# A gated decoder layer on one core: weight sums in halves of 512 KB, and a new place in memory for the tiles that TensorE reads

## The chip, the cores and the metric

The kernel runs on one core of one Trainium2 chip. The time is the device time of one execution in microseconds; the kernel before took 329.92 us (median of 3 runs, 329.75 to 330.6).

## The reference

One pre-norm decoder layer on 256 tokens of width 1024, in float32, with three branches side by side.

```python
h = rms_norm(x, norm_g[layer])
(qa, ka, va, ga, ub, vb, gb, qc, gc, ma, mb, mc) = split_cols(h @ w_in[layer], IN_SPLITS)
out_a = moba_attention(qa, ka, va) * jax.nn.silu(ga)          # 6 heads of 128, causal, partial rotary
out_b = gmlp_spatial_gate(ub, vb, ...) * jax.nn.silu(gb)      # 6 groups of 128 channels
out_c = memory_cross_attention(qc, mem_n, w_mem_kv[layer]) * jax.nn.silu(gc)   # 4 heads, 256 memory tokens
y = (jax.nn.sigmoid(ma) * (out_a @ w_branch_a[layer])
     + jax.nn.sigmoid(mb) * (out_b @ w_branch_b[layer])
     + jax.nn.sigmoid(mc) * (out_c @ w_branch_c[layer]))
x = x + y @ w_out[layer]
return rms_norm(x, final_norm_g)
```

The combined projection `w_in` is 1024 x 8704. With it come a memory projection (1024 x 1024), the three branch projections (2048 x 1024 together) and the output projection (1024 x 1024).

## The kernel before, in words

**Chunks.** All weights pass through TensorE as a row of chunks of 128 x 1024 float32. The list `PLAN` names them: `mvk` (memory keys and values), `tok` (some values by token), `fea` (features: queries, keys, gates), `st` (products, below), `br` (branch projections), and at the end `out`. Two chunks that follow each other are one piece of 128 x 2048, 1 MB.

**Split numbers.** Each matmul is made of several in a fast float32 format (fp32r). ScalarE copies a chunk into `hi` (L258), which rounds it; VectorE subtracts that from the chunk and gets `lo` (L262). `hi` and `lo` are rings of five chunks, the split is issued four chunks ahead of the matmuls (`LEAD`). Activations are split the same way: `n` (the normed input), `s` (sums of its blocks), `m` (memory), `ah`/`al`, `obh`/`obl`, `och`/`ocl` (the branches' outputs) and `y`. Each holds a high and a low part. A product of `x` and `w` is `xh*hi + xh*lo + xl*hi`. In `tok`, `st`, `br` and `out` the activation is the stationary operand and `hi` or `lo` streams past in 512 columns; in `fea` the weights are stationary and `n` streams, 512 columns for `hi` (high and low part side by side) and 256 for `lo`.

**Products.** For five groups of 1024 columns (`g` = 0 to 4) a 2 x 2 block scheme makes seven products instead of eight, in the order 1, 2, 5, 3, 6, 7, 4. The weights of a product are a block of the matrix or a sum of blocks, and stand in one of two buffers of 1 MB, `form0` and `form1` (for odd `g` the two change places). Products 1, 5, 6, 4 use one buffer one after the other: block 0 is loaded (L226, SP's queue), then blocks 1, 3 and 2 are added to it in turn. Products 2, 3, 7 use the other: blocks 2 and 3 are loaded, then block 1 is added. An addition is a DMA that accumulates into the buffer (L229, POOL's queue). For groups 0 to 2 product 6 is made otherwise: VectorE adds the other buffer, which holds block 3 for product 3, over all 2048 columns at once (L240). A load or an addition can start only when the product before it in the same buffer has been split, so it waits for the last `lo` of that chunk.

**Order.** The order is written by a small planner at build time (`Units`). The chunks set a beat; at each chunk the planner issues the DMAs due there (`dma`, by the chunk at which a buffer comes free, `free`), then small units of attention, norms and gates where an engine has room, then the split of the chunk four ahead, then the matmuls. Each engine then works through its own list in that order and waits on semaphores. Products 1 to 7 of groups 0 to 2 and the first three of group 3 stand between feature chunks. The last eleven stand between the branch chunks: after the first two `br` chunks products 3 and 6 of group 3, after the next two product 7, then 4 and (group 4) 1, then 2 and 5, then 3 and 6, then 7, then 4. Two `br` chunks are 24 matmuls.

**Where tiles begin.** Pools are laid out one after the other, each tile at a multiple of 32 bytes in a partition. In the built program the bytes at which the tiles begin are, modulo 128: `m`, `s`, `n`, `y`, `obh`, `obl`, `och`, `ocl` at 96 (between bytes 45664 and 92768), `ah` (113280), `al` (127616 and 133760), `hi` (160384) and `lo` (180864) at 0, `ones` at 64 and its partner `dg` at 0. The tile `wspb` of 3096 bytes is what sets the tiles behind it apart from those ahead of it. All offsets inside these tiles are multiples of 512 bytes.

Of the kernel before, what the change touches and what calls it, by code (L numbers as in the profile page):

```python
# [24 lines left out]
F32 = mybir.dt.float32  # L25
# [3 lines left out]
OP = mybir.AluOpType  # L29
# [55 lines left out]
class Units:  # L85
# [29 lines left out]

    def fits(self, u, i, pe, now):
        name, e, us, fn, after, wait, due = u
        due = min([due] + [self.pe[a] + 4 for a in after if a in self.pe])
        if pe != (e == PE) or any(a not in self.end for a in after):
            return False  # L120
        if i >= due or e is None:
            return True
        if pe:
            return self.ready(after) + self.margin <= now
        if e == QUEUE:

            return self.ready(after) <= now
        lead = 0.5 if e == POOL else max(0.3, self.room - (2.4 if e == ACT else 1.3) - self.ahead - us)
        return self.t[e] <= now + lead and self.ready(after) <= max(now, self.t[e]) + 0.3

    def slot(self, i, pe):

        now, u = self.t[PE], True
        while u:
            if pe:
                now = self.t[PE]
            u = next((u for u in self.todo if self.fits(u, i, pe, now)), None)
            if u:
                self.todo.remove(u)
                name, e, us, fn, after, wait, due = u  # L140
                if e == PE:
                    self.pe[name] = i
                at = self.ready(after)
                self.end[name] = (at if e is None else self.run(e, us, at)) + wait
                fn()
# [3 lines left out]
def tile_hybrid_layer(ctx: ExitStack, tc: tile.TileContext, mw, xT, mem, x, fin_g, ln_g, w, ws, w_sp, b_sp, rope, out):  # L149
# [30 lines left out]
        return slice(h * 128, (h + 1) * 128)  # L180


    RAW, SPL, LEAD, JT = 3, 5, 4, 2
    raw, hi, lo = {}, {}, {}
    chunks = []
# [23 lines left out]

    def load(j):  # L210
        raw_alloc(j)
        parts = 2 if 18 <= j < 47 else 1
        for i in range(parts):
            load_part(j, i * PIECE // parts, (i + 1) * PIECE // parts)

    def block(g, i):

        return bass.AP(tensor=ws.tensor, offset=ws.offset + (4 * g + i) * 128 * PIECE, ap=[[PIECE, 128], [1, PIECE]])

    def form_tile(i):  # L220
        if f"form{i}" not in V:
            V[f"form{i}"] = (wts if i == 0 else act).tile([128, PIECE], F32, name=f"form{i}", tag=("f0", "mr")[i])
        return V[f"form{i}"]

    def form_load(i, g, b):
        nc.sync.dma_start(form_tile(i), block(g, b))  # L226

    def form_add(i, g, b):
        nc.gpsimd.dma_start(form_tile(i), block(g, b), accum_op=OP.add)  # L229


    SUMS = (0, 1, 2)
    FORMS = {1: (0, 0), 5: (0, 1), 6: (0, 3), 4: (0, 2), 2: (1, 2), 7: (1, 1), 3: (1, 3)}

    def buf(g, i):
        return FORMS[i][0] ^ (g % 2)

    def form_sum(i, g, b):

        nc.vector.tensor_tensor(form_tile(i), form_tile(i), form_tile(1 - i), OP.add)  # L240
        U.run(DVE, 2.35)

    def form_step(g, i):

        if i == 6 and g in SUMS:
            return form_sum, buf(g, i), g, 3

        return (form_add if i in (5, 6, 4, 7) else form_load, buf(g, i), g, FORMS[i][1])

    def split_alloc(c):  # L250
        if "hi" not in V:
            for n in ("hi", "lo"):
                V[n] = wts.tile([128, SPL, CH], F32R, name=n, tag=n)
        hi[c], lo[c] = V["hi"][:, c % SPL, :], V["lo"][:, c % SPL, :]

# [438 lines left out]
        nc.sync.dma_start(V["lng"], rows(ln_g, BW))  # L694

    def load_wsp():
        t = slot_tile("wspb", [128, GB * 128 + GB], "trig")
        nc.sync.dma_start(t, w_sp)
        V["wsp"], V["bst"] = t[:, 0:GB * 128].rearrange("p (g t) -> p g t", g=GB), t[:, GB * 128:]

    def cut_wsp():
        for g in range(GB):
# [439 lines left out]
        nc.sync.dma_start(out[:, t, 512:D], z[:, 512:D])  # L1142


    dma, ready, free = {}, {}, [6, 9]
    for c in range(n_br):
        if chunks[c][0] == "st" and chunks[c][3] == 0:
            b = buf(*chunks[c][1:3])
            at = free[b] + (chunks[c][2] not in (5, 6, 4, 7))
            if chunks[c][2] == 6 and chunks[c][1] in SUMS:  # L1150
                at = free[1 - b]
            dma.setdefault(at, []).append(form_step(*chunks[c][1:3]))
            ready[c // 2] = at
            free[b] = c + 2 - LEAD
    pace = lambda c: 5.0 + sum(SPAN.get(k[0], 2.73) for k in chunks[:c])
    for c, at in ready.items():
        i = chunks[2 * c][2]
        ready[c] = pace(at) + (2.5 if i == 6 and chunks[2 * c][1] in SUMS else 10.0 if i in (4, 5, 6, 7) else 6.0)
    for c in range(n_br + 4):
        now[0] = c  # L1160
        if c == n_br:
            nc.scalar.preload_act_table(AF.Sqrt)
            residual_parts()
        if c == n_br - 8:
            load_x()
        s = c + (LEAD if c > 9 else 3)
        for fn, *args in dma.pop(c, []):
            fn(*args)
        U.room = sum(SPAN.get(k[0], 2.73) for k in chunks[c:c + LEAD])
        U.slot(c, False)  # L1170
        if c in (7, 8):
            split_lo(2 * c - 6)
            U.end[f"s{2 * c - 6}"] = U.run(DVE, 1.23, U.t[ACT])
        for e in {5: (), 6: (), 7: (9,), 8: (11,), 9: (12, 13)}.get(c, (s,) if s > 3 else ()):
            if chunks[e][0] == "st":
                raw[e // 2] = form_tile(buf(*chunks[e][1:3]))
                came = ready[e // 2]
            else:
                came = {4: 24.0, 5: 25.5}.get(e // 2, 0.0)
            (split_mvk if e < KD else split)(e)  # L1180
            U.end[f"s{e}"] = U.run(DVE, 1.23, U.run(ACT, 1.05, max(U.end.get(f"c{e - SPL}", 0), came)))
        if c in (6, 7):
            split_alloc(2 * c - 4)
            split_hi(2 * c - 4)
            U.run(ACT, 1.05, (23.5, 28.0)[c - 6])
        s += c == 9
        if s % 2 == 1 and s // 2 in PLAIN:
            q = PLAIN.index(s // 2) + 2
            if 4 < q < len(PLAIN):
                load(PLAIN[q])  # L1190
            if q == 6:
                load_mem()
        kind = chunks[c][0]
        U.end[f"c{c}"] = U.run(PE, SPAN.get(kind, 2.73), U.end.get(f"s{c}", 0.0))
        if kind == "mvk":
            mm_mvk(c)
        elif kind == "tok":
            mm_tok(c)
        elif kind == "fea":
            mm_fea(c)  # L1200
        elif kind == "br":
            mm_br(c)
        elif kind == "st":
            mm_st(c)
        else:
            mm_out(c, 0)
            for a, b in (((0, 256), (256, 512)) if chunks[c][1] else ((0, 512),)):
                mm_out(c, 1, a, b)
        U.slot(c, True)
# [115 lines left out]
```

## Time and profile before

| | |
|---|---|
| median of 3 runs | 329.92 us |
| the profiled execution | 333.19 us, its span 331.5 us |
| granted TensorE clock, mean | 0.979 |
| TensorE busy | 317.0 us, 96% of the span |
| VectorE busy | 255.5 us, 77% |
| ScalarE busy | 226.8 us, 68% |
| GpSimd busy | 25.0 us, 8% |
| moved by DMA | 77.24 MB |

The span reaches from the first to the last instruction; the execution's own time is 1.7 us longer. A row of a group gives the line, the engine, the operation, the tile written and the tiles read, then the number of instructions, their busy time, the mean of one, and the idle time of the engine just before them with what ended it. "PEld" is the loading of TensorE's stationary operand. Some matmul records are missing from a trace, so times between matmuls are taken from their starts.

### The profile page before, as it was taken

The page shows a single profiled execution, that of the slowest core. Times are in us where ns is not written, and L with a number is a line of the kernel's source. Part 1 is how long each engine was busy: PE and PEld are TensorE (multiplying, and loading weights), DVE is VectorE, ACT ScalarE, POOL GpSimd, SP SyncE. Part 2 cuts the span into 40 slices and gives each one's busy share as a digit, 9 for nine tenths or more (in the row PEclk, how much of TensorE's full clock was granted, in tenths as well). Part 3 has the DMA queues.
Part 4 walks back from the last instruction along what each step waited for, and adds up shares of the span by engine and source line. Part 5 has one row for each costly group of instructions (what it writes and reads, how often), then busy time and mean ns, then how long its engine had stood idle before and what let it go on. Part 6 is the DMA issues. An engine that isn't in the chain of part 4 may idle for free. (4 is left out here: it accounts for less than half of the span.)

```text
span 331.5 us, 4343 instructions
## 1 busy us (share of the span) xinstructions
PE 317.0 (96%) x1542; PEld 261.6 (79%) x1542; DVE 255.5 (77%) x369; ACT 226.8 (68%) x357; POOL 25.0 (8%) x42
## 2 busy tenths in 40 slices
PE   7999999999999999999999999989999897999992
PEld 3888888888888888888888888867887675878882
DVE  2889989977698986975986999846982939889532
ACT  3877979547977869779957967819672744487333
POOL 1000030020010011022011010111010111000022
PEclk9999999999999999999999999997999797999997
DMA  7999998669669489869659789898799697943003
GB/s 205 407 401 417 406 284 288 228 150 190 245 217 259 156 257 213 280 223 222 207 190 173 225 334 211 253 265 165 264 312 292 173 266 133 378 175 128 2 0 127
DMA packets 16294, 77.24 MB, mean 233 GB/s; under 512 B 2064, under 2 KB 3088, under 8 KB 9744
## 3 DMA queue, kind: packets, MB, share of 16 engines
q1 hardware_dynamic: 13680, 59.00, 48.3%
q0 software_dynamic: 2448, 17.83, 28.4%
q8 instruction: 12, 0.20, 0.2%
q10 hardware_dynamic: 144, 0.13, 0.1%
q14 instruction: 10, 0.08, 0.1%
HBM read 75.12 MB, written 1.05 MB: 230 GB/s over the span
## 5 line engine op out<-in xcount | busy, mean ns | idle before, releaser
L262 DVE TENSOR_TENSOR lo<-form,hi 128x1024 fp32r<-128x1024 f32 x70 | 84.1, 1219 | 35.9 <-ACT hi L258 35.5
L258 ACT ACTIVATE hi<-form 128x1024 fp32r<-128x1024 f32 x70 | 72.2, 1056 | 44.8 <-DMA form<-in_ws_dram 33.3
L262 DVE TENSOR_TENSOR lo<-raw,hi 128x1024 fp32r<-128x1024 f32 x58 | 70.0, 1221 | 12.6 <-ACT hi L258 12.2
L258 ACT ACTIVATE hi<-raw 128x1024 fp32r<-128x1024 f32 x58 | 60.8, 1058 | 14.1 <-PE acc L448 4.7
L628 PE MATMUL acc<-n,hi 128*128 128x512 f32 x240 | 61.3, 397 | 0.0
L628 PEld LDWEIGHTS acc<-n,hi 128*128 128x128 f32 x240 | 43.7, 188 | 9.0
L229 POOL DMA_DIRECT2D form<-in_ws_dram x17 | 14.9, 876 | 255.4 <-DVE lo L262 151.0
L568 PE MATMUL acc<-hi,s 128*128 128x512 f32 x96 | 33.1, 403 | 0.0
L628 PEld LDWEIGHTS acc<-n,lo 128*128 128x128 f32 x240 | 30.9, 188 | 1.5
L628 PE MATMUL acc<-n,lo 128*128 128x256 f32 x240 | 31.9, 283 | 0.0
L568 PE MATMUL aux<-hi,s 128*128 128x512 f32 x64 | 24.0, 440 | 2.5 <-ACT hi L258 2.5
L568 PE MATMUL acc<-hi,n 128*128 128x512 f32 x72 | 25.3, 408 | 0.0
L568 PEld LDWEIGHTS acc<-hi,s 128*128 128x128 f32 x96 | 18.0, 188 | 4.2
L568 PE MATMUL acc<-lo,s 128*128 128x512 f32 x48 | 18.9, 394 | 0.0
L568 PEld LDWEIGHTS aux<-hi,s 128*128 128x128 f32 x64 | 13.5, 211 | 6.5 <-ACT hi L258 3.3
L568 PE MATMUL aux<-lo,s 128*128 128x512 f32 x32 | 14.6, 457 | 3.9 <-DVE lo L262 3.9
L568 PE MATMUL aux<-hi,n 128*128 128x512 f32 x48 | 15.9, 395 | 0.0
L568 PEld LDWEIGHTS acc<-hi,n 128*128 128x128 f32 x72 | 13.5, 188 | 3.0
L568 PE MATMUL acc<-lo,n 128*128 128x512 f32 x36 | 14.2, 394 | 0.0
L568 PEld LDWEIGHTS aux<-lo,s 128*128 128x128 f32 x32 | 6.6, 206 | 6.9 <-DVE lo L262 5.5
L568 PEld LDWEIGHTS aux<-hi,n 128*128 128x128 f32 x48 | 9.0, 187 | 2.2
L568 PEld LDWEIGHTS acc<-lo,s 128*128 128x128 f32 x48 | 9.0, 188 | 1.9
(233 smaller groups left out, 578.9 us busy)
## 6 DMA issues: line engine op xcount, KB each, us to landing
raw<-in_w_dram SPq DMA_DIRECT2D x18, 1024.0 KB, 8.7
form<-in_ws_dram POOLq DMA_DIRECT2D x17, 1024.0 KB, 9.7
form<-in_ws_dram SPq DMA_DIRECT2D x15, 1024.0 KB, 5.0
raw<-in_w_dram SPq DMA_DIRECT2D x22, 512.0 KB, 7.2
st<-in_mw_dram SPq DMA_DIRECT2D x7, 384.0 KB, 7.5
raw<-in_w_dram SPq DMA_DIRECT2D x8, 256.0 KB, 7.3
xk<-in_x_dram SPq DMA_DIRECT2D x2, 512.0 KB, 7.5
xt<-in_xT_dram SPq DMA_DIRECT2D x2, 512.0 KB, 8.6
```

Of the source, the lines that this page charges most:

```text
L229: nc.gpsimd.dma_start(form_tile(i), block(g, b), accum_op=OP.add)
L258: nc.scalar.activation(hi[c][:, a:b], raw[c // 2][:, o + a:o + b], AF.Copy)
L262: nc.vector.tensor_tensor(lo[c][:, a:b], raw[c // 2][:, o + a:o + b], hi[c][:, a:b].bitcast(F32), OP.subtract)
L568: nc.tensor.matmul(p, x[:, k0 + k, tsl(t)], wt[c][:, a * 512:(a + 1) * 512], start=first and a + j == 0, stop=half == 1 and a + j == 3, sk ...
L628: nc.tensor.matmul(o, wt, m, start=i == 0, stop=i == len(passes) - 1, skip_group_check=True)
```

## The change

Four edits, all in one file.

1. **Sums by halves.** Every load and every addition of a `form` buffer is issued for 1024 columns (512 KB) at a time, each half as soon as that half of the buffer is free. Product 6 is made by VectorE in all five groups, in two halves of 1024 columns.
2. **Where tiles begin.** `wspb` gets 3200 bytes instead of 3096, so `ah`, `al` and `hi` now begin at 96 modulo 128, as `n`, `s`, `m`, `y`, `obh`, `obl`, `och`, `ocl` do. A pad of 64 bytes stands ahead of `lo`, which begins at 32 modulo 128, 64 bytes apart from the others (`LOPAD = 16` floats). `ones` stays at 64, `dg` moves to 32.
3. **The planner.** The due time of a unit that follows a matmul is bound differently, for ScalarE and TensorE units.
4. Raw weight pieces 47 and 48 are loaded in two parts as well.

```diff
     def fits(self, u, i, pe, now):
-        due = min([due] + [self.pe[a] + 4 for a in after if a in self.pe])
+        due = due if pe else min([due] + [int(self.pe[a]) + 4 for a in after if a in self.pe])
...
+                up = [self.pe[a] for a in after if a in self.pe and self.pe[a] % 1 == 0]
                 if e == PE:
                     self.pe[name] = i
+                elif up and e == ACT:
+                    self.pe[name] = up[0] + 0.5
...
+    LOPAD = 16
...
-        parts = 2 if 18 <= j < 47 else 1
+        parts = 2 if 18 <= j < 49 else 1
...
-    def form_load(i, g, b):
-        nc.sync.dma_start(form_tile(i), block(g, b))
-
-    def form_add(i, g, b):
-        nc.gpsimd.dma_start(form_tile(i), block(g, b), accum_op=OP.add)
-    SUMS = (0, 1, 2)
+    def form_half(i, h):
+        return form_tile(i)[:, h * CH:(h + 1) * CH]
+
+    def form_load(i, g, b, h):
+        nc.sync.dma_start(form_half(i, h), block(g, b, h))
+
+    def form_add(i, g, b, h):
+        nc.gpsimd.dma_start(form_half(i, h), block(g, b, h), accum_op=OP.add)
+
+    def form_sum(i, g, b, h):
+
+        nc.vector.tensor_tensor(form_half(i, h), form_half(i, h), form_half(1 - i, h), OP.add)
+        U.run(DVE, 1.23)
...
-        if i == 6 and g in SUMS:
-            return form_sum, buf(g, i), g, 3
-        return (form_add if i in (5, 6, 4, 7) else form_load, buf(g, i), g, FORMS[i][1])
+    HOW = {5: (form_add, 8.0), 7: (form_add, 8.0), 4: (form_add, 8.0), 6: (form_sum, 1.5)}
...
-            for n in ("hi", "lo"):
+            for n, pad in (("hi", 0), ("lo", LOPAD)):
+                if pad:
+                    wts.tile([128, pad], F32, name=n + "pad", tag=n + "pad")
                 V[n] = wts.tile([128, SPL, CH], F32R, name=n, tag=n)
...
-        t = slot_tile("wspb", [128, GB * 128 + GB], "trig")
-        nc.sync.dma_start(t, w_sp)
+        t = slot_tile("wspb", [128, GB * 128 + 32], "trig")
+        nc.sync.dma_start(t[:, 0:GB * 128 + GB], w_sp)
...
-    dma, ready, free = {}, {}, [6, 9]
+    dma, ready, free = {}, {}, [[6, 6], [9, 9]]
...
+        if chunks[c][0] == "st":
+            _, g, i, h = chunks[c]
+            b = buf(g, i)
+            fn, us = HOW.get(i, (form_load, 5.0))
+            at = free[1 - b][h] if i == 6 else free[b][h] + (i not in HOW)
+            dma.setdefault(at, []).append((fn, b, g, FORMS[i][1], h))
+            ready[c] = pace(at) + us
+            free[b][h] = c + 1 - LEAD
```

VectorE's list around products 3 and 6 of group 3, where `form_326` (`form0`) holds block 3 and `form_400` (`form1`) becomes the sum; before:

```order
L262 TENSOR_TENSOR lo<-form_326,hi 128x1024
L673 TENSOR_TENSOR ub<-ub,jt 128x512
L262 TENSOR_TENSOR lo<-form_326,hi 128x1024
L1023 TENSOR_TENSOR ub<-ub,mt_1768 128x512
L262 TENSOR_TENSOR lo<-form_400,hi 128x1024 x2
L262 TENSOR_TENSOR lo<-raw,hi 128x1024
```

and now (the buffers' numbers are 327 and 402; the split's line L262 is now L264):

```order
L675 TENSOR_TENSOR ub<-ub,jt 128x512
L264 TENSOR_TENSOR lo<-form_327,hi 128x1024
L240 TENSOR_TENSOR form_402<-form_402,form_327 128x1024
L264 TENSOR_TENSOR lo<-form_327,hi 128x1024
L240 TENSOR_TENSOR form_402<-form_402,form_327 128x1024
L1025 TENSOR_TENSOR ub<-ub,mt_1781 128x512
L264 TENSOR_TENSOR lo<-form_402,hi 128x1024 x2
```

Two half sums have come in, one behind each half of product 3.

VectorE's list around products 3 and 6 of group 4, where the buffers have changed places and four evictions of branch b (L1075, L1077) stand between the halves of product 6; before:

```order
L262 TENSOR_TENSOR lo<-form_400,hi 128x1024 x2
L262 TENSOR_TENSOR lo<-form_326,hi 128x1024
L1075 TENSOR_TENSOR sigs_1855<-acc,sigs_1855 128x512
L1077 TENSOR_TENSOR sig_1462<-sig_1462,sigs_1855 128x512
L1075 TENSOR_TENSOR sigs_1855<-acc,sigs_1855 128x512
L1077 TENSOR_TENSOR sig_1462<-sig_1462,sigs_1855 128x512
L262 TENSOR_TENSOR lo<-form_326,hi 128x1024
```

and now:

```order
L264 TENSOR_TENSOR lo<-form_402,hi 128x1024
L240 TENSOR_TENSOR form_327<-form_327,form_402 128x1024
L264 TENSOR_TENSOR lo<-form_402,hi 128x1024
L240 TENSOR_TENSOR form_327<-form_327,form_402 128x1024
L264 TENSOR_TENSOR lo<-form_327,hi 128x1024
L1077 TENSOR_TENSOR sigs_1890<-acc,sigs_1890 128x512
L1079 TENSOR_TENSOR sig_1480<-sig_1480,sigs_1890 128x512
```

The two half sums stand ahead of the evictions, as the splits of product 3 did.

In POOL's list 30 additions of 128x1024 stand where 17 of 128x2048 stood, the two halves of a product next to each other; the two additions for product 6 of groups 3 and 4 are gone. SP's list has 30 loads of 128x1024 for 15 of 128x2048, nearly all side by side.

More of the change, by code (lines that the diff above doesn't have):

```diff
@@ L211, in load, with block @@
         raw_alloc(j)
-        parts = 2 if 18 <= j < 47 else 1
+        parts = 2 if 18 <= j < 49 else 1
         for i in range(parts):
             load_part(j, i * PIECE // parts, (i + 1) * PIECE // parts)
-    def block(g, i):
-        return bass.AP(tensor=ws.tensor, offset=ws.offset + (4 * g + i) * 128 * PIECE, ap=[[PIECE, 128], [1, PIECE]])
+    def block(g, i, h):
+        return bass.AP(tensor=ws.tensor, offset=ws.offset + (4 * g + i) * 128 * PIECE + h * CH, ap=[[PIECE, 128], [1, CH]])
     def form_tile(i):
@@ L236, in buf @@
         return FORMS[i][0] ^ (g % 2)
[L238 to L243, printed above, removed]
-        if i == 6 and g in SUMS:
-            return form_sum, buf(g, i), g, 3
-        return (form_add if i in (5, 6, 4, 7) else form_load, buf(g, i), g, FORMS[i][1])
+    HOW = {5: (form_add, 8.0), 7: (form_add, 8.0), 4: (form_add, 8.0), 6: (form_sum, 1.5)}
     def split_alloc(c):
         if "hi" not in V:
-            for n in ("hi", "lo"):
+            for n, pad in (("hi", 0), ("lo", LOPAD)):
+                if pad:
+                    wts.tile([128, pad], F32, name=n + "pad", tag=n + "pad")
                 V[n] = wts.tile([128, SPL, CH], F32R, name=n, tag=n)
@@ L696, in load_wsp @@
     def load_wsp():
-        t = slot_tile("wspb", [128, GB * 128 + GB], "trig")
-        nc.sync.dma_start(t, w_sp)
-        V["wsp"], V["bst"] = t[:, 0:GB * 128].rearrange("p (g t) -> p g t", g=GB), t[:, GB * 128:]
+        t = slot_tile("wspb", [128, GB * 128 + 32], "trig")
+        nc.sync.dma_start(t[:, 0:GB * 128 + GB], w_sp)
+        V["wsp"], V["bst"] = t[:, 0:GB * 128].rearrange("p (g t) -> p g t", g=GB), t[:, GB * 128:GB * 128 + GB]
     def cut_wsp():
@@ L1142, in out_store @@
         nc.sync.dma_start(out[:, t, 512:D], z[:, 512:D])
-    dma, ready, free = {}, {}, [6, 9]
+    dma, ready, free = {}, {}, [[6, 6], [9, 9]]
+    pace = lambda c: 5.0 + sum(SPAN.get(k[0], 2.73) for k in chunks[:c])
     for c in range(n_br):
[L1147 to L1158, printed above, removed]
+        if chunks[c][0] == "st":
[6 more added lines that the diff above has]
+            free[b][h] = c + 1 - LEAD
     for c in range(n_br + 4):
@@ L1176, in tile_hybrid_layer @@
                 raw[e // 2] = form_tile(buf(*chunks[e][1:3]))
-                came = ready[e // 2]
+                came = ready[e]
             else:
```

## The prediction

> **What bounds the kernel now.** I read the busy times first, then the stretches of the span, the waits, the chain of waits, and TensorE's instructions in order of time.
>
> ```profile
> span 331.5 us, 4343 instructions
> PE 317.0 (96%) x1542; PEld 261.6 (79%) x1542; DVE 255.5 (77%) x369; ACT 226.8 (68%) x357; POOL 25.0 (8%) x42
> 20.00:40.00 20.00, 20.00 (x95) 16.43 (x94) 19.56 (x35) 16.31 (x27) 0.00 (x0) 1.00 1.01 408
> 40.00:220.00 180.00, 180.00 (x938) 152.90 (x937) 150.72 (x226) 135.14 (x228) 15.59 (x24) 1.00 0.81 232
> 220.00:280.00 60.00, 53.60 (x206) 41.36 (x205) 39.97 (x41) 36.98 (x40) 4.32 (x5) 0.91 0.86 231
> 280.00:326.00 46.00, 45.66 (x229) 37.91 (x228) 32.88 (x44) 23.95 (x36) 3.60 (x4) 1.00 0.41 142
> ```
>
> The last four rows are stretches: busy time of PE, weight loads, DVE, ACT, POOL, then the granted clock, the DMA share and GB/s. TensorE works without a gap at full clock from 20 to 220 us and from 280 us on. Only 220 to 280 us holds gaps: 60.00 - 53.60 = 6.40 us idle, and the clock at 0.91, which costs about 0.09 x 60 = 5.4 us more. So two things can shorten this kernel: filling those gaps (at most 11.8 us), and a shorter time per matmul.
>
> The gaps, from the waits (us in total, times, longest) and from TensorE in order of time:
>
> ```profile
> PE aux L568 <- DVE lo L262: 3.9, 4, 2.1
> PE aux L568 <- ACT hi L258: 2.5, 2, 1.5
> POOL form L229 <- DVE lo L262: 151.0, 11, 42.0
> ACT hi L258 <- DMA form<-in_ws_dram: 33.3, 12, 7.8
> ...
> 221.36 0.39 PE L568 MATMUL aux<-hi,s 128*128 128x512 f32 x1
> 223.27 0.50 PE L568 MATMUL aux<-hi,s 128*128 128x512 f32 x1 [1.52 <-ACT hi L258]
> 257.55 0.50 PE L568 MATMUL aux<-hi,s 128*128 128x512 f32 x1 [0.93 <-ACT hi L258]
> 275.92 0.50 PE L568 MATMUL aux<-lo,s 128*128 128x512 f32 x1 [2.11 <-DVE lo L262]
> ```
>
> The 6.4 us are all in the chunks of products. ScalarE's split waits for a DMA into `form`, and TensorE then waits for the split. By the plan the three places are product 6 of group 3 (221 us), 5 of group 4 (256 us) and 6 of group 4 (271 us), and all three weights are sums made by an accumulating DMA.
>
> ```profile
> 211.16 0.86 POOL L229 DMA_DIRECT2D form<-in_ws_dram  x1 [13.21 <-DVE jt L643]
> 244.02 0.86 POOL L229 DMA_DIRECT2D form<-in_ws_dram  x1 [17.18 <-DVE lo L262]
> 260.39 0.86 POOL L229 DMA_DIRECT2D form<-in_ws_dram  x1 [15.51 <-DVE lo L262]
> 222.16 2.01 ACT L258 ACTIVATE hi<-form 128x1024 fp32r<-128x1024 f32 x2 [7.77 <-DMA form<-in_ws_dram]
> 256.44 2.00 ACT L258 ACTIVATE hi<-form 128x1024 fp32r<-128x1024 f32 x2 [5.95 <-DMA form<-in_ws_dram]
> 269.76 2.01 ACT L258 ACTIVATE hi<-form 128x1024 fp32r<-128x1024 f32 x2 [5.94 <-DMA form<-in_ws_dram]
> form<-in_ws_dram POOLq DMA_DIRECT2D x17, 1024.0 KB, 9.7
> form<-in_ws_dram SPq DMA_DIRECT2D x15, 1024.0 KB, 5.0
> q1 hardware_dynamic: 13680, 59.00, 48.3%
> q0 software_dynamic: 2448, 17.83, 28.4%
> ```
>
> From issue to use these three took 222.16 - 211.16 = 11.0, 12.4 and 9.4 us. The accumulating queue q0 needs 28.4/17.83 = 1.59% of the span per MB, the plain queue 0.82%: an add costs the DMA engines twice a load.
>
> **The sums by halves.** Removed: two accumulating DMAs (product 6 of groups 3 and 4), that is two of the three gaps. In their place VectorE adds the two buffers in two halves each.
>
> ```profile
> L262 DVE TENSOR_TENSOR lo<-form,hi 128x1024 fp32r<-128x1024 f32 x70 | 84.1, 1219 | 35.9 <-ACT hi L258 35.5
> L240 DVE TENSOR_TENSOR form<-form,form 128x2048 f32<-128x2048 f32 x3 | 6.9, 2285 | 0.0
> 217.99 0.68 DVE L1023 TENSOR_TENSOR ub<-ub,mt 128x512 f32<-128x512 f32 x1
> 218.43 0.86 POOL L229 DMA_DIRECT2D form<-in_ws_dram  x1 [6.41 <-DVE lo L262]
> 240.11 1.23 DVE L262 TENSOR_TENSOR lo<-form,hi 128x1024 fp32r<-128x1024 f32 x1 [0.34 <-ACT hi L258]
> 258.81 0.51 PE L568 MATMUL aux<-lo,s 128*128 128x512 f32 x1 [0.76 <-DVE lo L262]
> ```
>
> A half sum lies between 2285/2 = 1.14 us and the 1.22 us of a subtraction of the same size. Ten of them are 11.4 to 12.2 us against 6.9 before, so VectorE gains about 5 us, 4.9 of which is the two new sums, and they fall into 220 to 280 us, where it is busy 39.97 of 60.
>
> First place (group 3): VectorE worked without a break up to 217.99 + 0.68 = 218.7. With two half sums ahead (2.4 us) the low part of the first half of product 6 runs from 221.1 to 222.3. TensorE without a gap wants it one matmul after 221.6, at 221.8: about 0.5 us stay as a wait, too short to slow the clock. Third place (group 4): the sums stand ahead of four evictions that wait for the end of the branch chunk, so the first half is split by then; I put 0 there.
>
> Second place (product 5 of group 4) stays a DMA add, but each half goes out as soon as its own half of product 1 is split. In the present trace the issue at 244.02 follows the second split; the first ended at 240.11 + 1.23 = 241.3. The first 512 KB then have 256.4 - 241.3 = 15 us where the whole MB took 12.4. The second half is issued when the whole is now, moves half, and is wanted 1.4 us later (6 matmuls of 0.233) than the first, whose product would begin at 256.5 behind two splits of 2.3 us: at about 255.6. If the DMA engines set the pace, it is done no later than the whole is now less the head start of 2.7 us, 253.7. Bounds: nothing left, or the whole gap kept (0.93 + 0.76 us idle and a third of the clock's 5.4, 3.5 us); the head start speaks for the lower end, and I take 0.3 us. The DMA page of the Trainium skill (DMA: Bandwidth & Descriptors, Anatomy of one DMA) fits a load at 2.0 us plus its bytes over 436 GB/s, an estimate of 4.4 us for a MB and 3.2 us for half: halving would save 1.2 us of the landing and not half of it; the row above has 5.0 us for the MB and no half.
>
> What is late next: product 7, whose add must now follow the sum that reads its buffer. In the present trace product 7 of group 3 is issued at 218.43; its halves would go out at about 218.5 and 220.7, wanted at 227.6 and 229.0 (product 6 from 221.6, 2.8 us, a branch pair of 24 x 0.23 = 5.5 us, less the 2.3 us of splits): 9.1 and 8.3 us for half a MB where a MB has 9.7. I add nothing. Queues: SP issues 30 half loads for 15 and POOL 30 half adds for 17; at 0.86 us an issue POOL gains 11 us and is 8% busy. Behind a half's wait on SP stand the same raw loads as before, and the second half's wait ends when the whole's did. DMA work falls by two adds.
>
> So 11.8 - 0.8 = 11.0 us of the gap stretch should go. Moved activations and scores, and one more raw load in two parts, change which of two ready items goes first on an engine with slack: 0.
>
> **Where the tiles begin.** Before, the stationary n, s, m, y, obh, och begin at 96 modulo 128, hi and lo at 0, as do ah and al. So one group of matmuls reads both operands at one byte modulo 128: those with ah and al. Their pace, beside the same code with other tiles:
>
> ```profile
> 237.70 0.39 PE L446 MATMUL acc<-hi,ah 128*128 128x512 f32 x1
> ...
> 242.24 0.40 PE L448 MATMUL acc<-hi,al 128*128 128x512 f32 x1
> 284.49 2.80 PE aux L568 x12
> 41.66 2.04 PE L628 MATMUL acc<-n,lo 128*128 128x256 f32 x16
> 43.54 0.62 PE L628 MATMUL acc<-n,hi 128*128 128x512 f32 x2
> 53.81 0.40 PE L390 MATMUL aux<-dg,ones 128*128 128x256 f32 x2
> 54.06 0.40 PE L568 MATMUL acc<-hi,n 128*128 128x512 f32 x1
> ```
>
> Twenty steps between the first two rows: 4.54/20 = 0.227 us. The twelve of the chain's row: 0.2333 us. The difference, 6.3 ns in 233, is there with ScalarE, VectorE and DMA all at work beside it, and the one thing I find that sets ah and al apart is where they begin. After the change n, s, y, hi, ah, al begin at 96 and lo at 32.
>
> Pairs with hi that gain: 280 of the products (rows L568), 240 features (L628), 80 of branches b and c, 64 of the output, 32 token matmuls: 696, counted in 512 columns; the start, which waits for DMAs, I leave out. 696 x 6.3 ns = 4.4 us. Pairs with lo: 140 + 120 + 40 + 32 + 16 = 348 that were 32 apart, and 24 of branch a that were 0 apart; now all are 64 apart. The only pair 64 apart in the trace is ones (64) with dg (0): two matmuls of 256 columns in 54.06 - 53.81 = 0.25 us, 0.12 to 0.125 each, where sixteen others of 256 columns take 1.88/16 = 0.1175. That makes 0.24 to 0.25 for 512 columns. Bounds for a lo pair: 0.227 (64 apart is as good as 0) and 0.250; with two matmuls behind the upper end I take 0.237. Then 348 x 3.7 ns + 24 x 10 ns = 1.5 us is lost, and the layout is worth -4.4 + 1.5 = -2.9 us; with the bounds, -6.6 and +2.0.
>
> VectorE, with 19.56 of 20 us at 20 to 40 us, could hold up a faster TensorE there, but only by the few tenths that the layout gains in that stretch; I leave it within the range.
>
> **Sum.** Span 331.5 - 11.0 - 2.9 = 317.6 us. The profiled execution took 333.19 us, 1.7 over its span, and lies 3.3 above the median of the runs, 329.92. The same distance gives 317.6 + 1.7 - 3.3 = 316.0 us.
>
> **Rivals.** (1) 64 apart is as good as 0: all pairs at 0.227. For it: nothing in the trace tells a period of 128 from one of 64, since 32 apart is both times apart. Against: the ones and dg row. Layout -6.6: 312.3 us.
>
> (2) The layout does nothing, and ah and al are quick for another reason (their place in memory, far above n and y). Against: tiles at 96 behave alike wherever they lie, and apart from ah (same line of code, mean ns of one):
>
> ```profile
> L447 PE MATMUL acc<-lo,ah 128*128 128x512 f32 x24 | 9.4, 390 | 0.0
> L447 PE MATMUL acc<-lo,och 128*128 128x512 f32 x16 | 6.3, 395 | 0.0
> L447 PE MATMUL acc<-lo,y 128*128 128x512 f32 x16 | 6.3, 395 | 0.0
> ```
>
> Span 331.5 - 11.0 = 320.5, so 318.9 us. The Trainium skill's page TensorE: Matmul & The Clock Gate (Step-by-step: what each phase is for) has two independent read ports, so that loading the next weights takes no read bandwidth from the running matmul; by that rule where the two begin cannot matter. The 0.227 against 0.2333 above speaks against it.
>
> (3) The gaps only move: the halves of products 5 and 7 land late, or the sums queue behind splits, and about 6 of 11.8 us come back. For it: DMAs already take 0.86 of the engines' time there, and an add needs up to 12.4 us. Span 331.5 - 6 - 2.9 = 322.6, so 321.0 us.
>
> (4) Slower: matmuls that stream or load lo collide 64 apart. It decides from the point where 372 pairs lose what the rest gains: 11.0 + 4.4 = 15.4 us, 41 ns each, a pace of 0.274. At 0.280 the sum is 372 x 46.7 ns = 17.4 - 15.4 = +2.0: 332 us. The upper bound from the row, 0.250, is well below that.
>
> **How the numbers follow.** Forecast 0.50, (1) 0.20, (2) 0.12, (3) 0.15, (4) 0.03. The forecast's own spread is 313.5 to 318.5 (lo pairs 0.230 to 0.243). The range goes to 309.5, for lo pairs quicker than any row shows, and to 321.5 for (3). Faster than 329.92 by over 0.3%, about what a measurement of this kernel can tell, comes out in all cases but (4): 0.96 faster, 0.02 same, 0.02 slower.
>
> **What would show it.** Gaps: TensorE busy nearly throughout from 220 us on with a clock of 1.00, no wait of ScalarE for `form` longer than 2 us ahead of product 6, and ten half sums near 1.2 us. Layout: the paces of hi and lo matmuls apart, in chunks of products: 0.227 after a hi, 0.237 after a lo; 12 matmuls in 2.76 us where they take 2.80. A pace of 0.233 throughout would make (2) right, 0.227 throughout (1). New waits of TensorE for `lo` between 20 and 220 us would show that VectorE has become the bound, which would undo the layout's part.

## The result, and the profile after

The changed kernel takes 319.67 us (median of 4 runs, 319.65 to 321.31) against 329.84 us (329.46 to 330.6) for the kernel before in the same comparison: a ratio of 0.9701, with an interval of 0.9666 to 0.9736. It is 3% faster. The profiled execution took 319.68 us with a span of 317.9 us. The prediction had 316.0 us and a span of 317.6.

The page of the changed kernel: span, busy times, the two large DMA queues, the half sums, ScalarE's splits, and the issues into `form` (KB each, then the median us from issue to landing).

```profile
span 317.9 us, 4440 instructions
PE 309.8 (97%) x1542; PEld 258.8 (81%) x1542; DVE 260.4 (82%) x376; ACT 228.4 (72%) x357; POOL 35.9 (11%) x55
q1 hardware_dynamic: 15984, 59.00, 52.8%
q0 software_dynamic: 4320, 15.73, 26.8%
L260 ACT ACTIVATE hi<-form 128x1024 fp32r<-128x1024 f32 x70 | 73.4, 1057 | 22.9 <-DMA form<-in_ws_dram 11.5
L240 DVE TENSOR_TENSOR form<-form,form 128x1024 f32<-128x1024 f32 x10 | 12.2, 1222 | 0.0
form<-in_ws_dram SPq DMA_DIRECT2D x30, 512.0 KB, 5.9
form<-in_ws_dram POOLq DMA_DIRECT2D x30, 512.0 KB, 8.3
```

PE is busy 7.2 us less (317.0 before), and the span is 13.6 us shorter: the rest, 6.4 us, is idle time that is gone, and a part of the 7.2 us is clock, not work. The stretches of the changed kernel show this (busy time of PE, weight loads, DVE, ACT, POOL, then granted clock, DMA share, GB/s):

```profile
40.00:220.00 180.00, 180.00 (x940) 153.48 (x939) 155.81 (x235) 141.23 (x234) 24.39 (x35) 1.00 0.84 231
220.00:270.00 50.00, 50.00 (x218) 40.56 (x217) 41.20 (x42) 33.05 (x37) 6.37 (x8) 1.00 0.96 254
```

From 220 us on, where TensorE was busy 53.60 of 60 us at a clock of 0.91, it is now busy without a break at 1.00. The DMA share rose to 0.96, and TensorE has no wait there. The row of ScalarE's splits above has 11.5 us of waits for `form` where there were 33.3 (the longest 2.6 us, before 7.8), and TensorE waits for none of these splits.

The layout's part is smaller. Twelve matmuls of a product in the chain of waits of the changed kernel (start, us, what):

```profile
271.07 2.77 PE aux L570 x12
279.39 2.77 PE aux L570 x12
```

2.80 us before, 2.77 now: 0.2308 us a matmul for 0.2333. Summed over TensorE's starts, the time lost beyond 0.2333 us for 512 columns was 4.1 + 2.4 + 5.8 = 12.3 us between 220 and 280 us before (in stretches of 20 us), and is none now. So of the 13.6 us of span about 12.4 are gaps with their clock, and 1.2 the layout.

### The profile page after: what moved, and what is told of

The parts are those of the page before. It is cut to its first block, busy times and chain, and to the rows that moved or that the text cites. A ratio compares the mean times of both kernels' runs of the same rounds, so it can differ in the third digit from the quotient of the medians.

```text
span 317.9 us, 4440 instructions
## 1 busy us (share of the span) xinstructions
PE 309.8 (97%) x1542; PEld 258.8 (81%) x1542; DVE 260.4 (82%) x376; ACT 228.4 (72%) x357; POOL 35.9 (11%) x55
## 4 chain that ended last, share of the span: by engine, by line
PE 96%; DMA 2%; ACT 1%; issue 0%; ACTq 0%; SPq 0%; DVE 0%
PE acc L630 26%; PE acc L570 18%; PE aux L570 12%; PE acc L450 6%; PE acc L449 6%; PE acc L448 6%; PE acc L508 4%; PE aux L502 3%; PE aux L781 2%; PE aux L481 2%; PE acc L481 2%; DMA raw<-in_w_dram 2%; PE aux L449 1%; PE aux L450 1%; PE aux L448 1%; PE aux L885 1%
## 5 line engine op out<-in xcount | busy, mean ns | idle before, releaser
L264 DVE TENSOR_TENSOR lo<-form,hi 128x1024 fp32r<-128x1024 f32 x70 | 84.9, 1222 | 17.2 <-ACT hi L260 16.6
L260 ACT ACTIVATE hi<-form 128x1024 fp32r<-128x1024 f32 x70 | 73.4, 1057 | 22.9 <-DMA form<-in_ws_dram 11.5
L264 DVE TENSOR_TENSOR lo<-raw,hi 128x1024 fp32r<-128x1024 f32 x58 | 70.0, 1223 | 10.3 <-ACT hi L260 10.2
L236 POOL DMA_DIRECT2D form<-in_ws_dram x30 | 26.2, 872 | 231.0 <-DVE lo L264 83.8
L570 PE MATMUL aux<-hi,s 128*128 128x512 f32 x64 | 20.9, 392 | 0.0
L570 PEld LDWEIGHTS aux<-hi,s 128*128 128x128 f32 x64 | 12.0, 188 | 2.8
L643 ACT ACTIVATE qk<-acc 128x256 f32<-128x256 f32 x12 | 4.7, 389 | 11.5 <-PE acc L630 11.5
L570 PE MATMUL aux<-lo,s 128*128 128x512 f32 x32 | 12.6, 394 | 0.0
L240 DVE TENSOR_TENSOR form<-form,form 128x1024 f32<-128x1024 f32 x10 | 12.2, 1222 | 0.0
```

Of the source, the lines that this page charges most:

```text
L236: nc.gpsimd.dma_start(form_half(i, h), block(g, b, h), accum_op=OP.add)
L240: nc.vector.tensor_tensor(form_half(i, h), form_half(i, h), form_half(1 - i, h), OP.add)
L260: nc.scalar.activation(hi[c][:, a:b], raw[c // 2][:, o + a:o + b], AF.Copy)
L264: nc.vector.tensor_tensor(lo[c][:, a:b], raw[c // 2][:, o + a:o + b], hi[c][:, a:b].bitcast(F32), OP.subtract)
L570: nc.tensor.matmul(p, x[:, k0 + k, tsl(t)], wt[c][:, a * 512:(a + 1) * 512], start=first and a + j == 0, stop=half == 1 and a + j == 3, sk ...
```

## Experiments

All kernels below compute the whole layer. The expectations name theories by letter and say themselves what each holds. Unless it is said otherwise, an edit is made to the changed kernel.

### The layout alone, and the sums alone

In the kernel before, only the two tiles are moved:

```diff
-            for n in ("hi", "lo"):
+            for n, pad in (("hi", 0), ("lo", 16)):
+                if pad:
+                    wts.tile([128, pad], F32, name=n + "pad", tag=n + "pad")
...
-        t = slot_tile("wspb", [128, GB * 128 + GB], "trig")
+        t = slot_tile("wspb", [128, GB * 128 + 32], "trig")
```

> The kernel before with the new places of the tiles alone (wspb of 3200 bytes, lo 64 bytes further on); the sums stay whole, product 6 of groups 3 and 4 a DMA add. Theory A, from the profile after: the layout is worth about 1.1 us, since the product chunks there run at about 231 ns a matmul and not 227, and the feature chunks as before: gaps stay between 220 and 280 us, time 328.7 us. Theory B, the prediction's: 2.9 us, 327.0 us. If addresses do nothing: 329.8 us and 0.2333 us a matmul everywhere.

In the changed kernel, the tiles stand where they stood before:

```diff
-    LOPAD = 16
+    LOPAD = 0
...
-        t = slot_tile("wspb", [128, GB * 128 + 32], "trig")
+        t = slot_tile("wspb", [128, GB * 128 + GB], "trig")
```

> The changed kernel with the old places of the tiles (wspb of 3096 bytes, no pad ahead of lo): the sums by halves and the planner's edits alone. Theory A: no gap from 220 us on, clock 1.00, 0.2333 us a matmul: 1.1 us over the changed kernel, 320.8 us. Theory B (layout worth 2.9): 322.6 us.

Layout alone: 328.72 us (12 runs, 327.33 to 330.68) against 329.92 (23 runs, 327.77 to 331.81), ratio 0.9967 (0.9937 to 0.9996). Sums alone: 320.92 us (6 runs, 320.59 to 321.22), ratio 0.9739 (0.9701 to 0.9777). The two parts add up: 1.2 us and 9.0 us make 10.2, and the change has 329.84 - 319.67 = 10.2.

With the layout alone the gaps stay, in this stretch of that kernel and in its waits; the chunk is at 2.77 us as in the changed kernel:

```profile
220.00:280.00 60.00, 53.22 (x222) 41.07 (x221) 43.13 (x44) 37.25 (x41) 4.33 (x5) 1.00 0.88 233
...
PE aux L570 <- DVE lo L264: 4.3, 4, 2.1
PE aux L570 <- ACT hi L260: 1.6, 2, 0.9
...
279.76 2.77 PE aux L570 x12
```

With the sums alone the gaps are gone and the chunk is back at 2.80 us:

```profile
220.00:280.00 60.00, 60.00 (x261) 48.45 (x260) 50.72 (x52) 39.32 (x43) 6.95 (x8) 1.00 0.95 267
...
271.99 2.80 PE aux L570 x12
```

The stretch of the layout alone shows one more thing. It has 60.00 - 53.22 = 6.78 us of idle time, more than the kernel before in its profile (6.40), and yet a clock of 1.00 where that had 0.91. The clock does not follow from the idle time alone. In the kernel before, in stretches of 2 us, it falls to half some 2 us after a gap:

```profile
222.00:224.00 2.00, 0.50 (x1) 0.19 (x1) 0.75 (x1) 1.84 (x2) 0.00 (x0) 1.00 1.07 221
224.00:226.00 2.00, 1.47 (x5) 1.25 (x6) 1.61 (x2) 1.97 (x3) 0.03 (x1) 0.85 0.96 201
226.00:228.00 2.00, 2.00 (x6) 1.54 (x5) 0.48 (x1) 2.00 (x4) 0.83 (x1) 0.50 0.80 98
228.00:230.00 2.00, 2.00 (x8) 1.49 (x8) 1.41 (x3) 2.00 (x4) 0.00 (x0) 0.79 0.70 131
```

That is (0.15 + 0.50 + 0.21) x 2 = 1.7 us lost behind one gap, and the profile of the kernel before has three such places (5.1 us in all). In the layout alone the same places have no such stretch. Twenty-three executions of the kernel before lie between 327.77 and 331.81 us; the profile that the prediction rests on, 333.19 us with a mean clock of 0.979, was slower than any of them. The clock goes with the time in the others too: of the 48 executions of the kernel before in all comparisons of these experiments, the 28 with a mean clock of 0.993 or more have a median of 328.5 us, the 20 at 0.990 or less one of 330.6 us.

### Which part of the sums does it

In the kernel before, product 6 is a sum on VectorE in all five groups, but whole, and all loads and additions stay whole:

```diff
-    SUMS = (0, 1, 2)
+    SUMS = (0, 1, 2, 3, 4)
```

> The kernel before with product 6 of groups 3 and 4 made by VectorE over 2048 columns at once, as in groups 0 to 2; loads and adds stay whole, places as before. If the two removed adds are what counts, the gaps at 221 and 271 us are gone and the one at 256 us (product 5 of group 4, idle 1.7 us and 1.7 us of clock) stays: about 322 to 323 us by the medians. If the halves are needed as well (a whole sum of 2.3 us stands ahead of both splits): gaps of 1 to 2 us at 221 and 271 us and 325 us or more.

In the changed kernel, product 6 of groups 3 and 4 is made by DMA additions again, in halves:

```diff
+    def how(g, i):
+        return (form_add, 8.0) if i == 6 and g > 2 else HOW.get(i, (form_load, 5.0))
...
-            fn, us = HOW.get(i, (form_load, 5.0))
-            at = free[1 - b][h] if i == 6 else free[b][h] + (i not in HOW)
+            fn, us = how(g, i)
+            at = free[1 - b][h] if fn is form_sum else free[b][h] + (i not in HOW)
```

> The changed kernel, layout and all, with product 6 of groups 3 and 4 made by DMA adds of 512 KB as products 5, 7 and 4 are, in place of VectorE's half sums. If halves alone fill the gaps: 319.7 us and no wait from 220 us on. If the adds that were taken away are needed (two more of 8 us in a stretch with the DMA engines 0.96 busy): the gaps at 221 and 271 us come back in part, idle 2 to 4 us and some of the clock, 322 to 325 us.

Whole sums: 326.57 us (10 runs, 325.62 to 329.27), ratio 0.9921 (0.9885 to 0.9958). Halves with the additions kept: 323.53 us (4 runs, 323.18 to 325.01), ratio 0.9832 (0.9771 to 0.9894). Neither reaches the kernel with both: the first, with the old places of the tiles, is to be held against the 0.9739 of the sums alone, the second, with the new places, against the 0.9701 of the changed kernel. Whole sums, the waits of TensorE in order of time:

```profile
224.83 0.50 PE L446 MATMUL acc<-hi,ah 128*128 128x512 f32 x1 [0.19 <-ACT hi L258]
226.09 0.50 PE L447 MATMUL acc<-lo,ah 128*128 128x512 f32 x1 [0.76 <-DVE lo L262]
255.93 0.60 PE L568 MATMUL aux<-hi,s 128*128 128x512 f32 x1 [1.86 <-ACT hi L258]
257.19 0.79 PE L568 MATMUL aux<-lo,s 128*128 128x512 f32 x1 [0.66 <-DVE lo L262]
```

The gaps ahead of product 6 are gone but for 0.3 us at 221 (one of 0.95 us has come up in branch a at 225), and the gap ahead of product 5 of group 4, which remains a whole DMA addition, has grown to 1.86 + 0.66 = 2.5 us. Behind it the matmuls are 0.427 us apart for 6.8 us, at half the clock. So the first alternative had the places right and its 322 to 323 us wrong: the gap that was to stay did not stay as it was. With halves and additions it is the other way round, the gap ahead of product 5 is gone and those ahead of product 6 are there, at 222 and 266 us; its stretch has the DMA share at 1.01:

```profile
222.70 0.51 PE L574 MATMUL aux<-hi,s 128*128 128x512 f32 x1 [0.27 <-ACT hi L264]
223.97 0.50 PE L574 MATMUL aux<-lo,s 128*128 128x512 f32 x1 [0.75 <-DVE lo L268]
266.78 0.50 PE L574 MATMUL aux<-hi,s 128*128 128x512 f32 x1 [1.06 <-ACT hi L264]
268.04 0.50 PE L574 MATMUL aux<-lo,s 128*128 128x512 f32 x1 [0.77 <-DVE lo L268]
...
220.00:270.00 50.00, 47.16 (x201) 37.11 (x199) 36.84 (x38) 32.80 (x36) 8.66 (x10) 1.00 1.01 267
```

So each half of this part removes its own gaps: the sums those of product 6, the halves that of product 5. In the kernel with whole sums TensorE, no longer held up at 221 us, comes to product 5 earlier and waits longer there, so the two are worth more together. The planner's edits and the two parts of pieces 47 and 48 are in every kernel here that has the halves and in none with whole loads; no run shows what they do by themselves.

### At which distance do the places matter

The layout gave 1.2 us, not 2.9. First, `lo` is put at the same byte modulo 128 as all others:

```diff
-    LOPAD = 16
+    LOPAD = 0
```

> The changed kernel with lo at the same byte modulo 128 as hi and the activations (no pad). If pairs 0 apart run at the 0.227 us of branch a before, whatever stands beside them: 1140 matmuls of 512 columns gain 4 to 6 ns on the changed kernel, 5 to 6 us, 314 us, and all chunks of products take 2.72 us for 12. If 64 apart is as good as 0 apart: the changed kernel's 319.7 us. If the quick pace of branch a is a cadence that mixed streams don't reach: 319 to 321 us with product chunks at 2.77 to 2.80 us.

320.64 us (7 runs, 320.22 to 324.53), ratio 0.9736 (0.9693 to 0.9779): the same as the sums alone. The profiled execution is the slowest of the seven, 324.53 us: the half additions of product 5 of group 4 came late in it (ScalarE waits 5.1 us for one), and TensorE waits 2.2 us there and 0.9 us at product 6. The halves do not close that gap in every execution. All tiles begin at 96 modulo 128, and the chunk is at 2.80 us:

```profile
275.65 2.80 PE aux L570 x12
```

"At one byte modulo 128" is therefore not what made `ah` and `al` quick. In bytes modulo 256 the kernel before has `n`, `s`, `y` and the branches b and c at 96, and `ah`, `al`, `hi`, `lo` at 128. Here `ah`, `al`, `hi`, `lo` are at 224 and the others at 96, 128 apart, and again only the pairs with `ah` and `al` run at 0.2275 us. Two readings were left: the period is 256 bytes or longer, or the tiles have to lie in one region of memory. So everything was put at 96 modulo 256, then at one byte modulo 512 and modulo 1024, by the length of `wspb` (832, 896, 1024 floats):

```diff
-    LOPAD = 16
+    LOPAD = 0
...
-        t = slot_tile("wspb", [128, GB * 128 + 32], "trig")
+        t = slot_tile("wspb", [128, 832], "trig")
```

> The changed kernel with wspb of 3328 bytes and no pad ahead of lo: all tiles that TensorE reads (ones and the score tiles apart) begin at 96 modulo 256, while n and hi stay 256 apart modulo 512. Branch a (ah with hi, a whole multiple of 2048 bytes apart in every kernel that had 0.227 us) keeps 0.227. Theory P (the relative place counts, with a period of 256): n, s, y and the rest come to 0.227 as well, product chunks 2.72 us for 12, and 314 to 315 us, a kernel faster than both. Theory Q (a longer period): 0.233 for n, s, y, 320.7 us. Theory R (ah and al are quick by their own region of memory): 0.233 and 320.7 us here and in the next two.

> As the one before with wspb of 3584 bytes: all at 96 modulo 512, n and hi 512 apart modulo 1024. P: 0.227 us, 314 to 315 us. Q with a period of 512: 0.227 here for the first time; with a longer one 0.233 still. R: 0.233, 320.7 us.

> As the one before with wspb of 4096 bytes: all at 608 modulo 1024. P and Q with a period up to 1024: 0.227 us and 314 to 315 us. R: 0.233, 320.7 us.

At one byte modulo 256: 318.97 us (316.88 to 319.57), ratio 0.9691 (0.9622 to 0.9761). Modulo 512: 317.36 us (316.18 to 318.42), 0.9635 (0.9573 to 0.9697). Modulo 1024: 316.66 us (316.05 to 318.06), 0.9621 (0.9560 to 0.9682). The kernel before took 328.5 us in the same comparison. The chunk of a product, from the chain of the first:

```profile
268.85 2.72 PE aux L570 x12
```

and of the last:

```profile
122.50 2.72 PE acc L570 x12
268.70 2.72 PE aux L570 x12
```

2.72/12 = 0.2267 us, with the pairs that had 0.2333 before and wherever they lie: the period is 256 bytes, and the region does not matter. The larger periods add nothing to the pace; the three times overlap, and in the three profiled executions what differs is a gap of 0.3 to 1.3 us near 261 us (by TensorE's starts). The pace came as theory P had it; the 314 to 315 us did not. The 240 matmuls of 512 columns in the features came to 0.229 us only (table below), those of 256 columns became a little slower, and these gaps came up.

Then only `lo` was moved, by 32, 64 and 128 bytes, everything else at one byte modulo 1024:

```diff
-    LOPAD = 16
+    LOPAD = 8
...
-        t = slot_tile("wspb", [128, GB * 128 + 32], "trig")
+        t = slot_tile("wspb", [128, 1024], "trig")
```

(`LOPAD` 8, 16 and 32 in the three.)

> The kernel with all tiles at one byte modulo 256 (wspb of 4096 bytes), but lo 32 bytes further. If each matmul is priced by its own pair: matmuls with hi keep 0.2275 us, those with lo go to the 0.233 that 32 apart had before; 372 x 5.5 ns = 2 us over that kernel, 318.7 us. If the cadence breaks as a whole when every third stream stands elsewhere: all at 0.231 to 0.233 and 319 to 321 us.

> The same with lo 64 bytes further, the distance of the change, with hi in the place where it gains. Own-pair price: hi 0.2275, lo between 0.227 and 0.240, the price that the prediction had to guess. Cadence breaks: all at 0.231 to 0.233, as in the changed kernel, 319 to 320 us.

> The same with lo 128 bytes further. The changed kernel with lo beside hi had hi and lo 128 apart from the activations and 0.233 us throughout. Own-pair price: hi 0.2275, lo 0.233, 318.7 us. Cadence breaks: all near 0.231 to 0.233.

32 bytes: 320.3 us (319.34 to 322.29), ratio 0.9734 (0.9677 to 0.9790). 64: 319.1 us (318.72 to 320.36), 0.9694 (0.9656 to 0.9732). 128: 319.54 us (318.26 to 321.31), 0.9705 (0.9653 to 0.9756). The chunk in the chain of each, in this order:

```profile
271.65 2.78 PE aux L570 x12
```

```profile
270.12 2.80 PE aux L570 x12
```

```profile
281.16 2.75 PE aux L570 x12
```

(Earlier chunks of the kernel with 64 bytes are at 2.77.) The mean distance from the start of a matmul to that of the next (ns; distances over 250 left out), by the pair of tiles of the first, over the whole trace:

| pair, columns | before | after | `lo` with `hi`, 224 | all at 96 (1024) | `lo` +32 | `lo` +64 | `lo` +128 |
|---|---|---|---|---|---|---|---|
| `n`, `hi`, 512 (products) | 233.2 | 231.2 | 232.6 | 227.7 | 230.5 | 231.1 | 228.7 |
| `s`, `hi`, 512 | 233.0 | 230.7 | 232.8 | 227.5 | 231.1 | 231.7 | 227.9 |
| `s`, `lo`, 512 | 233.0 | 231.9 | 232.6 | 227.4 | 233.2 | 232.1 | 233.0 |
| `ah`, `hi`, 512 | 227.9 | 230.5 | 227.5 | 226.0 | 232.0 | 231.2 | 226.7 |
| `ah`, `lo`, 512 | 227.3 | 231.9 | 227.2 | 227.0 | 233.0 | 232.2 | 234.0 |
| `n`, `hi`, 512 (features) | 232.9 | 232.5 | 232.6 | 228.9 | 230.3 | 230.0 | 229.2 |
| `n`, `lo`, 256 (features) | 118.7 | 118.4 | 119.6 | 120.0 | 118.9 | 117.7 | 120.8 |
| `y`, `hi`, 256 | 116.5 | 119.6 | 118.7 | 119.3 | 117.0 | 117.5 | 117.9 |

With `lo` 128 bytes off, the pairs with `hi` keep their 227 to 229 ns and those with `lo` pay 233. With 32 or 64 off the pairs with `hi`, which have not moved against each other, become slower too, 230 to 232 ns. So 0 and 128 side by side leave each of these pairs its own price, and 32 and 64 beside 0 spoil the matmuls around them. The rule is not complete. In the changed kernel, `obh` and `och` with `hi`, 128 apart, are at 228 ns, beside pairs with `lo` at 233; and with `lo` 128 bytes off, the output's `y` with `hi`, 0 apart, is at 232 ns and `y` with `lo` at 230. What in TensorE does this, no run shows.

### The best version again

The kernel with all tiles at one byte modulo 1024 (`wspb` of 1024 floats, `LOPAD = 0`), in more executions:

> The kernel with all tiles at one byte modulo 256 (wspb of 4096 bytes, no pad) once more, for a narrower interval: product chunks at 0.2275 us a matmul, no gap or one under 1 us near 260 us, 316 to 318 us, a ratio of 0.960 to 0.966; the changed kernel's was 0.970. Were its lead chance, 0.970 again.

317.39 us (6 runs, 316.17 to 319.05) against 329.23 (11 runs, 327.3 to 330.6), ratio 0.9633 (0.9588 to 0.9677). Its ten runs in the two comparisons lie at 316.05 to 319.05 us, those of the changed kernel at 319.65 to 321.31, though the two were not run beside each other. The profiled execution here had two gaps; that of the first comparison had none at the first place and 0.3 us at the second. The stretch, the waits, TensorE's two waits, what ScalarE waited for ahead of the first, and VectorE ahead of the second:

```profile
220.00:280.00 60.00, 58.08 (x254) 47.16 (x254) 49.30 (x52) 37.82 (x41) 5.45 (x7) 1.00 0.89 259
...
PE aux L570 <- DVE lo L264: 1.9, 2, 1.2
...
251.61 0.50 PE L570 MATMUL aux<-lo,s 128*128 128x512 f32 x1 [0.76 <-DVE lo L264]
263.94 0.50 PE L570 MATMUL aux<-lo,s 128*128 128x512 f32 x1 [1.16 <-DVE lo L264]
...
249.24 1.06 ACT L260 ACTIVATE hi<-form 128x1024 fp32r<-128x1024 f32 x1 [1.46 <-DMA form<-in_ws_dram]
...
262.06 0.69 DVE L1079 TENSOR_TENSOR sig<-sig,sigs 128x512 f32<-128x512 f32 x1
262.67 1.22 DVE L264 TENSOR_TENSOR lo<-form,hi 128x1024 fp32r<-128x1024 f32 x1
...
270.81 2.72 PE aux L570 x12
```

A quicker TensorE calls for the weights earlier, and two things then come late. At 250 us it is the second half addition of product 5 of group 4. At 262 us it is VectorE, which works without a break: the low part of the second half of product 6 stands behind four evictions of branch b (L1077, L1079) and ends at 263.9, where TensorE wanted it at 262.6. In the changed kernel that low part ended at 263.8 and was wanted at 264.2, so there were only 0.4 us to spare. By TensorE's starts the two gaps cost this execution 2.6 us; whether they also make the spread of the others, 316.17 to 319.05, one trace does not show.

## Why the prediction was right, and where it was not

**The gaps: right, a little low.** The step "11.8 - 0.8 = 11.0 us of the gap stretch should go" measured 12.4 us in the profile, more than the 11.8 that the prediction took for the most that could go. The 0.8 us that were to stay did not: at product 6 of group 3 the prediction had VectorE working without a break to 218.7, the first low part of that product coming at 222.3, and TensorE 0.5 us late. VectorE's instructions of the changed kernel in order of time:

```profile
213.84 1.22 DVE L240 TENSOR_TENSOR form<-form,form 128x1024 f32<-128x1024 f32 x1
214.97 1.22 DVE L264 TENSOR_TENSOR lo<-form,hi 128x1024 fp32r<-128x1024 f32 x1
216.11 1.22 DVE L240 TENSOR_TENSOR form<-form,form 128x1024 f32<-128x1024 f32 x1
217.25 0.69 DVE L1025 TENSOR_TENSOR ub<-ub,mt 128x512 f32<-128x512 f32 x1
217.85 1.22 DVE L264 TENSOR_TENSOR lo<-form,hi 128x1024 fp32r<-128x1024 f32 x1
219.57 1.22 DVE L264 TENSOR_TENSOR lo<-form,hi 128x1024 fp32r<-128x1024 f32 x1 [0.50 <-ACT hi L260]
```

Both half sums and all that the prediction left ahead of them end by 217.9, and the first low part at 219.1; VectorE even waits 0.5 us for ScalarE. The prediction gave the planner's reordering 0 ("changes which of two ready items goes first"). Here the new order is the likely reason that the 0.5 us did not stay. Two groups of small work, in the kernel before

```profile
196.99 1.65 DVE L967 SCALAR_TENSOR_TENSOR ut<-aux,wspb,ut 128x256 f32<-128x256 f32 x4
199.69 1.28 DVE L981 TENSOR_TENSOR mid<-mid,gc 128x512 f32<-128x512 f32 x2
```

and in the changed kernel

```profile
190.63 1.29 DVE L983 TENSOR_TENSOR mid<-mid,gc 128x512 f32<-128x512 f32 x2
193.30 1.66 DVE L969 SCALAR_TENSOR_TENSOR ut<-aux,wspb,ut 128x256 f32<-128x256 f32 x4
```

run 4 to 9 us earlier, and are 2.9 us of work. The experiment with whole sums, in the old order, still lost 0.3 us at this place. The half sums themselves, 1.222 us, are at the upper end of the 1.14 to 1.22 given.

**Product 5 of group 4: right in this execution.** The prediction argued from the head start of the first half. Its two additions are these two rows of POOL in the changed kernel, where the kernel before issues the whole at 244.02 us:

```profile
235.28 0.86 POOL L236 DMA_DIRECT2D form<-in_ws_dram  x1 [13.25 <-DVE lo L264]
237.71 0.86 POOL L236 DMA_DIRECT2D form<-in_ws_dram  x1 [1.57 <-DVE lo L264]
```

No wait of TensorE stands behind them. Some 4 of these 6 to 9 us are the gap at 221 us, which is gone ahead of them. Counted to the split of product 2, the next on ScalarE (248.01 before, 243.14 now), the halves are issued 3.9 and 1.4 us earlier than the whole was. They land little sooner: after a median of 8.3 us (accumulated) where a whole MB had 9.7, and plain half loads after 5.9 us where a MB had 5.0. The estimate of 3.2 us for half a MB that the prediction worked out from the Trainium skill (DMA: Bandwidth & Descriptors, Anatomy of one DMA) is well below the 5.9 us measured here. The page gives its fit for DMAs issued from GpSimd, and the 5.9 us are those of SP; no run has a plain half load from GpSimd. So what the halves gain at product 5, where the experiment that kept the additions has no gap either, comes mostly from the earlier issue. The margin is thin: with `lo` beside `hi` and in the best version, one execution each waited there again (2.2 and 0.8 us).

**The layout: right in sign by luck, its size wrong by more than a half.** The term -2.9 us measured -1.2; twelve matmuls took 2.77 us for the 2.76 forecast, but at 0.231 after a `hi` and 0.232 after a `lo`, not at 0.227 and 0.237, and the features hardly moved. The step that failed is "one group of matmuls reads both operands at one byte modulo 128". It was the only thing that the prediction found to set `ah` and `al` apart, but they were also at one byte modulo 256, and that is what counts. After the change `n` and `hi` are 128 apart modulo 256, and `ah` and `hi` 0 apart. So the 696 pairs with `hi` did not gain 6.3 ns each: 280 of the products gained 2.2 (0.6 us for the 1.8 in the sum), 240 of the features 0.4 (0.1 us for 1.5). The 348 pairs with `lo` did not lose 3.7 ns each, they gained 0 to 1. That the sum came out as a gain is luck. The move that was to gain, `hi`, `ah` and `al` to 96 modulo 128, is worth nothing that could be measured where `lo` moves along (0.9736 against the 0.9739 of the old places). The gain came only with the 64 bytes of `lo`, which the prediction had put down as a loss of 1.5 us. The row of `ones` and `dg`, the sole witness for the price of 64 bytes, was two matmuls of 256 columns, and carried over badly: `lo` 64 apart costs 232 ns, not 237. Branch a lost 0.3 us where 0.24 were predicted, but not as predicted: its 24 pairs with `lo` lost 4.6 ns for the 10, and its 48 with `hi`, 0 apart before and after, lost 2.6 and 5.0 ns where no loss was forecast. The bounds of the term, -6.6 and +2.0, held it.

**The rule on the ports.** Of the second rival the prediction said that by the page TensorE: Matmul & The Clock Gate of the Trainium skill (Step-by-step: what each phase is for) places cannot matter, since loading the next weights takes no read bandwidth from the running matmul. The same program with the same instructions at 0.2333 and 0.2267 us, by the length of one tile, speaks against that conclusion for this number format; which of the two readings is held up, no run shows.

**From span to time: wrong by 3.3 us.** The span came out at 317.9 for 317.6, by luck: the gaps gave 1.4 us more than forecast, the layout 1.7 us less. The time came out at 319.67 for 316.0. The step that failed is "the same distance gives 317.6 + 1.7 - 3.3". The profiled execution of the kernel before had three stretches of half clock behind its gaps, 5.1 us. The layout alone, with as much idle time and a clock of 1.00 in that stretch, had a span of 326.6 us, and 327.8 with the 1.2 us of the layout added back: 3.7 below the 331.5. By TensorE's starts it lost 8.9 us in its gaps where that execution lost 12.3. Both differences are about the size of the 3.3 us. A kernel without the gaps has none of that, so nothing was left to subtract: its profile and its median are 319.68 and 319.67. In medians the gaps are therefore worth 9.0 us (sums alone), not the 12.4 of that one profile. Had the prediction left 317.6 + 1.7 = 319.3 us standing, it would have been 0.4 us off, with the same luck in the span. Not all of the spread of the kernel before is shown to be clock: single executions of it at a mean clock of 0.999 had spans of 326.1 and of 328.9 us, so the lengths of the gaps vary as well.

**The rivals.** The first (64 apart as good as 0) falls with the pace of `lo` at 64, 232 ns. The second (the layout does nothing) was nearest in time, 318.9 us, but with the same 3.3 us wrongly taken off: the kernel that it describes, the sums alone, took 320.92 us, and the layout alone is at 0.9937 to 0.9996. The third (gaps move) did not happen in the changed kernel; in part it did in single executions of its variants, where product 5's halves landed late and product 6 queued on VectorE (3.9 us lost with `lo` beside `hi`, 2.6 us in the best version). The fourth (lo pairs at 0.274 us or more) had nothing to it: no pair of 512 columns is above 0.235.

## What to carry to other kernels

Where one profiled execution lies above the median of the runs, ask what in it is chance, and whether the change removes that: a distance to the median that comes from clock lost behind gaps must not be taken over to a kernel that has no gaps. A period found from one group of quick instructions is only known down to the distances that the trace holds, so list the operands' places modulo several powers of two before naming one. A transfer that arrives late is helped first by issuing its first half earlier, and by taking a competing transfer away; it took both here.

## What the runs showed of the hardware that was not expected

- TensorE's fp32r matmuls of 512 columns take 0.226 to 0.229 us when all stationary and moving tiles begin at one byte modulo 256 (the first chunks, with `m`, up to 0.232), and mostly 0.232 to 0.234 us where they are 32 or 128 bytes apart and none is 64 apart. Distances of 32 or 64 bytes in some pairs slow their neighbours, which are 0 apart, to 0.230 to 0.233.
- Matmuls of 256 columns go the other way: 0.120 us against 0.1187 in the features, 0.1193 against 0.1165 in the output. Over 240 and 48 of them this takes back some 0.4 us of the best version's gain, and is not explained.
- After a gap the clock can be at half for 3.4 us (twice the 1.7 us lost, above), or stay at 1.00 after gaps of the same size: 6.40 us idle in 60 with a clock of 0.91, and 6.78 us idle with 1.00.
